# Placing on-chip buffers by their start address modulo 256 bytes in a two-layer encoder trunk

## The chip, the core and the metric

The kernel runs on one core of a Trainium2 chip. The metric is the device time of one execution in microseconds (us); lower is better. TensorE (PE) multiplies, VectorE (DVE) and ScalarE (ACT) work on elements, GpSimd (POOL) and SyncE (SP) mostly issue DMAs. A matmul has two operands in the on-chip memory: a stationary one of 128 columns, which a weight load (PEld) brings into the array first, and a moving one of up to 512 columns, which then streams through it. In a row of the trace "out<-moving,stationary" is the order.

## The reference

One even and one odd layer on 1024 tokens of width 1024, all in float32, cut to what matters:

```python
def even_mixer(x, ...):          # layer 0
    c_q, c_kv, k_r, f = split(x @ w_in)
    q = rms_norm(c_q) @ w_uq;  k, v = rms_norm(c_kv) @ (w_uk, w_uv)     # 8 heads
    p = softmax((q_nope @ k_nope.T + rot(q_rope) @ rot(k_r).T) * scale)
    return concat([p @ v, fft2(f).real]) @ w_out
def odd_mixer(x, ...):           # layer 1
    u, v = split(gelu(x @ w_in))
    s = einsum('gpq,bnqgc->bnpgc', w_s, chunks(layer_norm(v))) + b_s
    return (u * s) @ w_out
for layer in range(2):
    x = layer_norm(alpha * x + mixer(x))
    x = layer_norm(alpha * x + (silu(x @ w_gate) * (x @ w_up)) @ w_down)
```

## The kernel before

Every float32 operand is split into a high and a low part (`split`, one ACT copy and one DVE subtraction) and every product is made of three matmuls (`mm3`: high by high, high by low, low by high). The big products use a seven-product block scheme (`seven`, `reduce`, `v_pair`).

The stages follow each other in time: the input projection (`even_front`, 0 to 139 us of the profiled span), the Fourier part and the attention (139 to 570), `reduce` of the mixer, the feed-forward of layer 0 (`ffn`, 712 to 1137), its `reduce`, the v half (`v_pair`, 1372 to 1532) and the u half (`spatial`, 1532 to 1757) of layer 1, its `reduce`, the feed-forward of layer 1 (1934 to 2359) and the last `reduce`.

Tiles come from pools, which are stacked from the left end of the memory upwards (`side` "left") or from the right end downwards; what is opened earlier shifts what is opened later. The start addresses modulo 256, as the built program has them, are the same on every partition. "Gap" below is the moving operand's start minus the stationary one's, modulo 256.

| matmuls | stage | moving at | stationary at | gap |
|---|---|---|---|---|
| 3648 of `xo`/`xa` by `whi`/`wlo` of pool wts, 512 columns | feed-forward, u half | 32 | 160 | 128 |
| 720 of the same by `whi`/`wlo` of pool wtx | feed-forward | 32 | 32 | 0 |
| 3000 of `xo` by `xo` | `reduce` | 32 | 32 | 0 |
| 312 of `cq`/`ckv` by `whi`/`wlo` | attention | 32 | 160 | 128 |
| 480 of `xT` by `whi`/`wlo` | input projection | 224 | 160 | 64 |
| 48 of `whi`/`wlo` by `gh`/`gl`, 512 columns (and a few by `gm`) | Fourier | 160 | 192 | 224 |
| 384 of `kh`/`kl` by `qh`/`ql` | scores (L1242) | 224 | 224 | 0 |
| 256 of `krh`/`krl` by `qs` | scores (L1242) | 32 | 224 | 64 |
| 768 of `pth`/`ptl` by `vh`/`vl`, 256 columns | probabilities by values | 224 | 224 | 0 |
| 1104 of `whi`/`wlo` by `xo`/`xa`, 256 columns | v half (L847) | 160 | 32 | 128 |
| 336 of the same with pool wtx | v half (L847) | 32 | 32 | 0 |
| 192 of `whi`/`wlo` by `ckv`, 256 columns | values | 160 | 32 | 128 |
| 512 transposes, stationary `p` | attention (L1261) | 128 | 224 | 160 |

In the feed-forward stages and the v half weight pairs are dealt in turn from five, one of pool wtx and four of pool wts (`more_weights`, `wpair`); the u half takes pool wts alone (`less_weights`). One unit of `seven` takes four pairs: three for two products each, the fourth for one, of twelve matmuls each.

Of the kernel before, what the change touches and what calls it, by code (L numbers as in the profile page):

```python
# [9 lines left out]
F32 = mybir.dt.float32  # L10
# [5 lines left out]
P = 128  # L16
# [18 lines left out]
def tables():  # L35
    inv = np.float32(1.0) / (np.float32(10000.0) ** (np.arange(0, ROPE, 2, dtype=np.float32) / np.float32(ROPE)))
    ang = np.arange(S, dtype=np.float32)[:, None] * inv.astype(np.float32)[None, :]
    c, s = np.cos(ang).T, np.sin(ang).T
    rope_c = np.concatenate([c, c, c, c], 0).astype(np.float32)
# [22 lines left out]
def layouts(i):  # L62
# [5 lines left out]
    def cols(w, width=P, kn=8):  # L68

        k, n = w.shape  # L70
        w = w.reshape(k // (kn * P), kn, P, n // width, width).transpose(3, 0, 2, 1, 4)
        return c(w.reshape(-1, P, kn * width))
# [16 lines left out]
        "w_in": cols(w_in),  # L89
        "g_q": c(f["even_q_norm"][0].reshape(3, P).T),  # L90
        "g_kv": c(f["even_kv_norm"][0].reshape(2, P).T),
        "w_uqr": c(rope),
# [4 lines left out]
        "o_v": cols(o_in[:, SGU:], 256, 4),  # L97
        "o_gT": c(f["odd_sgu_norm_g"][0].reshape(16, P).T),
        "o_bT": c(f["odd_sgu_norm_b"][0].reshape(16, P).T),
        "o_ws": c(f["odd_w_spatial"][0].transpose(2, 0, 1).reshape(P, 8 * P)),  # L100
# [12 lines left out]
class Trunk:  # L113
# [8 lines left out]
    def pool(self, name, side, bufs=1):  # L122
        return self.tc.tile_pool(name=self.name(name), bufs=bufs, side=side, reuse_waits="tile")


    def sub(self, out, a, b):
        self.nc.vector.tensor_tensor(out, a, b, op=ALU.subtract)  # L127
# [91 lines left out]
    def run(self):  # L219
        tc, nc, a = self.tc, self.nc, self.a  # L220
        with ExitStack() as top:
            dr = top.enter_context(tc.tile_pool(name="dram", bufs=1, space=bass.MemoryType.DRAM))
            cp = top.enter_context(self.pool("const", "left"))
            self.open_weights(top, 3, 4)
            self.small = top.enter_context(self.pool("small", "left", bufs=4))
            self.ident = cp.tile([P, P], F32, name="ident")
            make_identity(nc, self.ident)
            self.ones = cp.tile([P, P], F32, name="ones")
            nc.vector.memset(self.ones, 1.0)
            nc.scalar.copy(self.small.tile([P, 1], F32, tag="nm", name="warm"), self.ones[:, 0:1])  # L230
            self.mhalf = cp.tile([P, 8], F32, name="mhalf")
            nc.vector.memset(self.mhalf, -0.5)
            D_ = lambda n, s, k: [dr.tile(s, F32, name=f"{n}{i}") for i in range(k)]
            mix = D_("mix", [P, S], 12)
            xs = [D_(f"xs{k}_", [P, D], NT) for k in range(3)]
            self.stage = {}

            def stage(n, W, H):
                k = len(W) // 2
                self.stage[n] = {"W": W, "H": H, **{x: D_(f"{n}{x}_", [P, D], k) for x in ("SA", "SB", "TA", "TB")}}  # L240
            order = [8, 9, 10, 11, 0, 1, 2, 3, 4, 5, 6, 7]
            stage("mix", [a["w_out"][k] for k in order], [mix[k] for k in order])
            stage("odd", [a["o_out"][j] for j in range(16)], D_("tp", [P, S], 16))
            for l in range(2):
                stage(f"ffn{l}", [a["w_down"][l, j] for j in range(22)], D_(f"h{l}_", [P, S], 22))
            self.vd = D_("vd", [P, NT, 256], 8)
            self.ahead = None
            with ExitStack() as fs:
                self.ps = fs.enter_context(tc.tile_pool(name="psum", bufs=2, space=bass.MemoryType.PSUM, reuse_waits="tile"))
                self.even_front(mix)  # L250
            with ExitStack() as ms:
                self.pb = ms.enter_context(tc.tile_pool(name="psumb", bufs=1, space=bass.MemoryType.PSUM, reuse_waits="tile"))
                self.turns, self.stamp = 0, [0] * 8
                self.wx = ms.enter_context(self.pool("wtx", "left"))
                self.rcycle, self.rcount = [(self.wp, self.wbufs[0])] * self.wbufs[0] + [(self.wx, 1)], 0
                xp = ms.enter_context(self.pool("xops", "left"))
                self.xo = tuple(xp.tile([P, 5, 2, 4, 256], F32R, name=f"xo{x}") for x in "hl")
                self.xa = None
                self.mp = ms.enter_context(self.pool("main", "right"))
                x_in = [a["x"][t * P:(t + 1) * P, :] for t in range(NT)]  # L260
                gate_up = lambda l: lambda j: (a["w_gate"][l, j], a["w_up"][l, j])
                w0 = {}

                def pre(l):
                    self.less_weights()
                    w0[l] = [self.right_operands(*gate_up(l)(0))]
                    self.more_weights()
                    w0[l].append(self.right_operands(*gate_up(l)(1)))

                def pre_v():  # L270
                    self.less_weights()
                    w0["v"] = self.v_begin(0)
                    self.more_weights()
                G = self.stage
                pend = self.reduce(G["mix"], x_in, None, (0, 0), xs[0], self.ahead, lambda: pre(0))
                self.ffn(w0[0], gate_up(0), G["ffn0"], pend)
                pend = self.reduce(G["ffn0"], xs[0], (0, 0), (0, 1), xs[1], None, pre_v)
                left = self.spatial(w0["v"], G["odd"], pend)
                pend = self.reduce(G["odd"], xs[1], (0, 1), (1, 0), xs[2], None, lambda: pre(1), left)
                self.ffn(w0[1], gate_up(1), G["ffn1"], pend)  # L280
                self.reduce(G["ffn1"], xs[2], (1, 0), (1, 1), None)
                self.xpool.__exit__(None, None, None)
# [617 lines left out]
    def even_front(self, mix):  # L900
        nc, a = self.nc, self.a
        col = lambda i: self.unit(a["w_in"][i], 8)
        with ExitStack() as keep:
# [7 lines left out]
            gq = cn.tile([P, 3], F32, name="gq")  # L911
            gkv = cn.tile([P, 2], F32, name="gkv")
            with ExitStack() as fs:
                fp = fs.enter_context(self.pool("fefo", "left"))
                fe = [fp.tile([P, 512], F32, name=f"fe{i}") for i in range(FG)]
                fo = [fp.tile([P, 512], F32, name=f"fo{i}") for i in range(FG)]
# [154 lines left out]
    def fourier(self, fe, fo, f512, chan, mix):  # L1071
# [2 lines left out]
        nc, a = self.nc, self.a  # L1074
        H = FD // 2
        with ExitStack() as es:
            gp = es.enter_context(self.pool("gf", "right"))
            T = lambda shape, dt, name: gp.tile(shape, dt, name=self.name(name))
            pair = lambda shape, name: (T(shape, F32R, name + "h"), T(shape, F32R, name + "l"))
# [89 lines left out]
    def attention(self, cq, ckv, kr, rc, rs, mix):  # L1169
        nc, a = self.nc, self.a  # L1170
        with ExitStack() as es:
            ap = es.enter_context(self.pool("attn", "right"))
            T = lambda shape, dt, tag, bufs=1: ap.tile(shape, dt, tag=tag, name=self.name(tag), bufs=bufs)
            st = {}

            def weights(hp):

                st[hp] = {"ur": self.unit(a["w_uqr"][hp], 3), "un": self.unit(a["w_uqn"][hp], 3), "ukv": self.unit(a["w_ukv"][hp], 2)}
# [116 lines left out]
            for i in range(len(items) + 3):  # L1295
# [6 lines left out]
                if i < len(items):  # L1302
# [7 lines left out]
                    left = max(1, NT - 1 - qt)  # L1310
# [24 lines left out]
```

## Time and profile before

| what | value |
|---|---|
| median of three runs | 2599.66 us (2596.24 to 2603.76) |
| profiled execution | 2598.74 us, of which the span of its instructions 2597.0 us |
| mean granted TensorE clock | 0.981 |
| busy: PE, PEld, DVE, ACT, POOL | 96%, 80%, 71%, 41%, 12% of the span |
| matmuls | 12294 |

The page's busy share of PE counts modelled ends, which overlap the next start; how long a matmul holds the engine is read from the starts of those that follow each other without idle time.

### The profile page before, as it was taken

To read this page: it belongs to the slowest core of one execution; us is meant where nothing else is said; L and a number is where in the kernel's file an instruction comes from. 1 tells how busy PE (TensorE), PEld (TensorE's weight loads), DVE (VectorE), ACT (ScalarE), POOL (GpSimd) and SP (SyncE) were. 2 spreads that over 40 slices of the span, in tenths; PEclk is the share of its full clock that TensorE was granted. 3 is DMA by queue.
4 is the path that set the end of the run, shared out by engine and by line. 5 is a ranking of instruction groups with operands and counts; after the bars stand their busy time and mean duration, and the time that the engine had idled before them with its cause. 6 is when DMAs were issued, how large, how long until landed. Compare 5 with 4: busy or idle time off the path is not lost. (4 is left out here: it accounts for less than half of the span.)

```text
span 2597.0 us, 33135 instructions
## 1 busy us (share of the span) xinstructions
PE 2491.1 (96%) x12294; PEld 2087.2 (80%) x12294; DVE 1841.1 (71%) x2673; ACT 1077.2 (41%) x1643; POOL 309.3 (12%) x504
## 2 busy tenths in 40 slices
PE   8989999989899999999999999898999999998997
PEld 7878888877778888878889997776877888887886
DVE  4448878757886666668687867788787666666767
ACT  4225555544643333334356432232474333333332
POOL 1000111010111111110011223230010101111001
PEclk9989999999999999999999999999999999999998
DMA  4122333148343454477645644476624534538654
GB/s 172 42 87 70 137 114 110 53 152 287 117 143 141 171 179 149 151 285 249 202 163 187 218 158 147 138 251 237 230 105 146 179 137 170 184 140 320 204 185 142
DMA packets 164073, 431.95 MB, mean 166 GB/s; under 512 B 19880, under 2 KB 26696, under 8 KB 163912
## 3 DMA queue, kind: packets, MB, share of 16 engines
q1 hardware_dynamic: 108216, 232.11, 27.1%
q0 software_dynamic: 55696, 197.73, 20.4%
q8 instruction: 96, 1.57, 0.3%
q14 instruction: 65, 0.53, 0.1%
HBM read 286.64 MB, written 138.41 MB: 164 GB/s over the span
## 5 line engine op out<-in xcount | busy, mean ns | idle before, releaser
L137 PE MATMUL b<-xoh,whi 128*128 128x512 f32 x1040 | 413.9, 398 | 20.1 <-ACT whi L131 18.2
L131 ACT CAST xoh<-rx 128x1024 fp32r<-128x1024 f32 (+1 forms) x264 | 255.0, 1006 | 424.6 <-PE b L138 323.2
L132 DVE TENSOR_TENSOR xol<-rx,xoh 128x1024 fp32r<-128x1024 f32 (+1 forms) x264 | 299.5, 1160 | 165.8 <-ACT xoh L131 165.1
L138 PE MATMUL b<-xol,xoh 128*128 128x512 f32 x1000 | 394.6, 395 | 19.3 <-DVE xol L132 19.3
L139 PE MATMUL b<-xoh,wlo 128*128 128x512 f32 x1040 | 411.1, 396 | 0.6 <-DVE wlo L132 0.2
L138 PE MATMUL b<-xol,whi 128*128 128x512 f32 x1040 | 410.8, 395 | 0.0
L137 PE MATMUL b<-xoh 128*128 128x512 f32 x1000 | 390.0, 396 | 21.5 <-ACT xoh L131 21.5
L131 ACT CAST whi<-raw 128x1024 fp32r<-128x1024 f32 (+3 forms) x265 | 250.5, 953 | 373.8 <-PE b L138 220.1
L132 DVE TENSOR_TENSOR wlo<-raw,whi 128x1024 fp32r<-128x1024 f32 (+3 forms) x265 | 290.0, 1101 | 162.9 <-ACT whi L131 160.1
L139 PE MATMUL b<-xoh,xol 128*128 128x512 f32 x1000 | 392.9, 393 | 0.0
L137 PEld LDWEIGHTS b<-xoh,whi 128*128 128x128 f32 x1040 | 196.9, 189 | 65.7 <-ACT whi L131 19.2
L137 PEld LDWEIGHTS b<-xoh 128*128 128x128 f32 x1000 | 190.0, 191 | 63.3 <-ACT xoh L131 24.0
L138 PEld LDWEIGHTS b<-xol,xoh 128*128 128x128 f32 x1000 | 190.5, 190 | 62.5 <-DVE xol L132 23.1
L139 PEld LDWEIGHTS b<-xoh,wlo 128*128 128x128 f32 x1040 | 196.6, 189 | 48.4 <-DVE wlo L132 3.7
L138 PEld LDWEIGHTS b<-xol,whi 128*128 128x128 f32 x1040 | 197.0, 189 | 44.4 <-issue 0.2
L139 PEld LDWEIGHTS b<-xoh,xol 128*128 128x128 f32 x1000 | 190.3, 190 | 39.9
L613 ACT COPY y<-b 128x512 f32<-128x512 f32 x200 | 116.7, 588 | 226.7 <-PE b L139 221.4
L137 PE MATMUL b<-xah,whi 128*128 128x512 f32 x416 | 166.2, 399 | 0.0
L138 PE MATMUL b<-xal,whi 128*128 128x512 f32 x416 | 165.2, 397 | 0.0
L139 PE MATMUL b<-xah,wlo 128*128 128x512 f32 x416 | 163.5, 394 | 0.0
L127 DVE TENSOR_TENSOR raw<-raw,raw 128x512 f32<-128x512 f32 (+1 forms) x172 | 126.9, 738 | 25.9 <-DMA raw<-w_up 21.4
L658 DVE TENSOR_TENSOR y<-b,y 128x512 f32<-128x512 f32 x84 | 57.9, 690 | 102.0 <-PE b L139 102.0
(376 smaller groups left out, 4523.6 us busy)
## 6 DMA issues: line engine op xcount, KB each, us to landing
raw<-w_gate SPq DMA_DIRECT2D x44, 512.0 KB, 3.5
raw<-w_up SPq DMA_DIRECT2D x44, 512.0 KB
q<-w_down POOLq DMA_DIRECT2D x44, 512.0 KB, 4.9
h<-x POOLq DMA_DIRECT2D x44, 512.0 KB, 3.7
rx<-h SPq DMA_DIRECT2D x66, 256.0 KB, 3.0
rx<-w_down SPq DMA_DIRECT2D x66, 256.0 KB, 5.1
raw<-o_v SPq DMA_DIRECT2D x16, 512.0 KB, 4.9
x<-o_out POOLq DMA_DIRECT2D x16, 512.0 KB, 6.2
```

Source lines behind the costliest of these rows:

```text
L127: self.nc.vector.tensor_tensor(out, a, b, op=ALU.subtract)
L131: a = self.nc.scalar.copy(hi, src)
L132: return a.ins, self.nc.vector.tensor_tensor(lo, src, hi.bitcast(F32), op=ALU.subtract).ins
L137: mm(ps, lh, rh, start=start, stop=False, skip_group_check=skip)
L138: mm(ps, lh, rl, start=False, stop=False, skip_group_check=skip)
L139: mm(ps, ll, rh, start=False, stop=stop, skip_group_check=skip)
L613: nc.scalar.copy(t, ps)
L658: self.last_v = nc.vector.tensor_tensor(sb, ps, sb, op=op).ins
```

## The change

The pool `small` is opened ahead of the weights' pool wts, so wts starts 128 bytes further on modulo 256. A helper `shift` takes a tile of n bytes that nothing uses, and clears it once on POOL; seven such tiles move what is placed after them.

```diff
+    def shift(self, pool, n):
+        self.nc.gpsimd.memset(pool.tile([P, n // 4], F32, tag=self.name("pad"), name=self.name("pad"), bufs=1), 0.0)
...
             cp = top.enter_context(self.pool("const", "left"))
+            self.small = top.enter_context(self.pool("small", "left", bufs=4))
             self.open_weights(top, 3, 4)
-            self.small = top.enter_context(self.pool("small", "left", bufs=4))
...
             with ExitStack() as fs:
+                self.shift(fs.enter_context(self.pool("top", "right")), 224)
...
         with ExitStack() as es:
+            self.shift(es.enter_context(self.pool("gap", "right")), 96)
             gp = es.enter_context(self.pool("gf", "right"))
...
         with ExitStack() as es:
+            self.shift(es.enter_context(self.pool("top", "right")), 192)
             ap = es.enter_context(self.pool("attn", "right"))
-            T = lambda shape, dt, tag, bufs=1: ap.tile(shape, dt, tag=tag, name=self.name(tag), bufs=bufs)
+            pads = {"kh0": 32, "vh": 64, "qh1": 160, "kh1": 32}
             st = {}
+
+            def T(shape, dt, tag, bufs=1):
+                n = pads.pop(tag, 0)
+                if n:
+                    self.shift(ap, n)
+                return ap.tile(shape, dt, tag=tag, name=self.name(tag), bufs=bufs)
```

In the built program the starts modulo 256 are then: `whi`/`wlo` of both pools 32, `xT` 0, `q` and `qs` 0, `k` 32, `pt` 32, `v` 96, `p` 96, `gh` 128; `xo`, `xa`, `cq`, `ckv` and `kr` stay at 32. So the gap is 0 for all 4368 matmuls of the feed-forward and u stages, for the 312 of `cq`/`ckv`, all 1440 of the v half and the 192 of the values; 32 for all 640 of the scores; 224 for the 480 of `xT`; 192 for the 768 of the probabilities by the values; 160 for those of `gh`; 32 for the transposes of `p`.

The order of instructions on PE, DVE, ACT and SP is what it was. On POOL the seven clears are new. Its rows around the Fourier part and the first pair of heads, before (`altf` is the Fourier part's first load, `rw` the rotated query half that the first scores need):

```order
L1085 DMA altf_1158<-t_alt 1x16x32
L1086 DMA altcf_1160<-t_altc 128x2
L330 DMA raw_1754<-w_out 128x1024
L330 DMA raw_1755<-w_out 128x1024
L1035 TENSOR_TENSOR rw_1445<-rw_1445,rope_s 128x512
```

The same place with the change; the clear of 24 columns waits for PE, as the load behind it did before, and the one of 40 columns waits for a matmul of the Fourier part:

```order
L127 MEMSET pad_1157 128x24
L1091 DMA altf_1168<-t_alt 1x16x32
L1092 DMA altcf_1170<-t_altc 128x2
L334 DMA raw_1779<-w_out 128x1024
L334 DMA raw_1780<-w_out 128x1024
L127 MEMSET pad_1529 128x8
L127 MEMSET pad_1551 128x16
L127 MEMSET pad_1643 128x40
L127 MEMSET pad_1707 128x8
L1040 TENSOR_TENSOR rw_1462<-rw_1462,rope_s 128x512
```

One clear now stands ahead of the Fourier part's loads and four ahead of the first product with `rw`; the other two stand near the program's start.

## Rows read from the trace of the kernel before

**Rows 1.** Stretches: length, then busy us and instructions by engine, granted clock, DMA.
```profile
core 0: us, PE busy (x) PEld busy (x) DVE busy (x) ACT busy (x) POOL busy (x), PEclk, DMA share, GB/s
139.00:570.00 431.00, 423.06 (x2553) 369.62 (x2552) 314.44 (x492) 209.72 (x398) 42.89 (x65) 0.98 0.29 94
712.00:1137.00 425.00, 423.90 (x1824) 344.20 (x1825) 293.07 (x405) 165.49 (x238) 46.42 (x87) 1.00 0.44 156
1372.00:1532.00 160.00, 155.50 (x1279) 154.41 (x1278) 120.50 (x193) 74.62 (x115) 39.05 (x70) 0.98 0.60 205
1532.00:1757.00 225.00, 207.23 (x981) 170.31 (x981) 174.06 (x344) 71.64 (x103) 62.02 (x94) 0.96 0.49 172
```

**Rows 2.** Timeline of PE in one feed-forward unit: start us, length us, instruction.
```profile
876.22 0.39 PE L137 MATMUL b<-xoh,whi 128*128 128x512 f32 x1
...
881.66 0.40 PE L137 MATMUL b<-xoh,whi 128*128 128x512 f32 x1
...
889.80 0.40 PE L139 MATMUL b<-xoh,wlo 128*128 128x512 f32 x1
```

**Rows 3.** Waits of ACT in the feed-forward of layer 0: total, times, longest.
```profile
ACT whi L131 <- PE b L138: 106.2, 55, 2.2
```

**Rows 4.** Timeline of PE in the attention, products of cq.
```profile
226.44 0.39 PE L137 MATMUL mm<-cq0h,whi 128*128 128x512 f32 x1
...
230.38 0.39 PE L139 MATMUL mm<-cq2h,wlo 128*128 128x512 f32 x1
```

**Rows 5.** Timeline of PE in the v half.
```profile
1480.69 0.28 PE L847 MATMUL b<-whi,xoh 128*128 128x256 f32 x1
...
1486.43 0.28 PE L847 MATMUL b<-whi,xoh 128*128 128x256 f32 x1
...
1492.01 0.28 PE L847 MATMUL b<-whi,xol 128*128 128x256 f32 x1
```

**Rows 6.** Timeline of PE in the Fourier part.
```profile
153.27 0.40 PE L138 MATMUL S<-wlo,gh 128*128 128x512 f32 x1
...
158.40 0.40 PE L139 MATMUL S<-whi,gl 128*128 128x512 f32 x1
```

**Rows 7.** Timeline of PE in one block of scores and the instruction after it.
```profile
389.77 0.39 PE L1242 MATMUL S<-kl,qh 128*128 128x512 f32 x1
...
391.87 0.40 PE L137 MATMUL mm<-ckv0h,whi 128*128 128x512 f32 x1
```

**Rows 8.** Timeline of PE in the input projection.
```profile
57.95 0.40 PE L138 MATMUL mm<-xT,whi 128*128 128x512 f32 x1
...
68.48 0.39 PE L139 MATMUL mm<-xT,wlo 128*128 128x512 f32 x1
```

**Rows 9.** Timeline of PE, probabilities by values.
```profile
394.50 0.28 PE L137 MATMUL mm<-pth,vh 128*128 128x256 f32 x1
...
396.90 0.28 PE L139 MATMUL mm<-pth,vl 128*128 128x256 f32 x1
```

**Rows 10.** Groups by line and form: count, busy us and mean ns, idle before.
```profile
L132 DVE TENSOR_TENSOR xol<-rx,xoh 128x1024 fp32r<-128x1024 f32 x236 | 281.2, 1216 | 153.3 <-ACT xoh L131 152.7 <-DMA rx<-mix 0.2
L132 DVE TENSOR_TENSOR wlo<-raw,whi 128x1024 fp32r<-128x1024 f32 x203 | 246.8, 1221 | 146.4 <-ACT whi L131 143.6 <-PE b L359 1.1
L1261 PE MATMUL mm<-ident,p 128*128 128x128 f32 x512 | 66.1, 272 | 0.0
L137 PEld LDWEIGHTS mm<-pth,vh 128*128 128x128 f32 x256 | 48.7, 190 | 0.9 <-ACT pth L131 0.5 <-DVE ptl L132 0.4
L359 PE MATMUL b<-ident,x 128*128 128x128 f32 x120 | 15.3, 273 | 0.4 <-DVE q L436 0.4
```

**Rows 11.** Timeline of POOL at the start and at the first rw product.
```profile
0.74 0.20 POOL masks.py:197 MEMSET ident<- 128x128 f32 x1 [0.29 <-POOLq L1327]
177.99 1.26 POOL L1035 TENSOR_TENSOR rw<-rw,rope_s 128x512 f32<-128x512 f32 x1 [23.89 <-DMA rw<-rt]
```

**Rows 12.** Timeline of PE at the end of the Fourier part.
```profile
159.62 0.28 PE L1137 MATMUL mm<-gl,altc 128*2 128x256 f32 x1
```

## The prediction

> **What bounds the kernel now.** I read the stretches first, then the starts of single matmuls, then the waits. In the feed-forward of layer 0 PE is busy 423.90 of 425.00 us, in the attention 423.06 of 431.00, in the v half 155.50 of 160.00 and in the u half 207.23 of 225.00; DVE and ACT are well below it in each, the DMA share is at most 0.60 [rows 1]. Where ACT stands idle in the feed-forward, it is mostly for PE to free a weight pair: 106.2 us in 55 waits [rows 3]. So the time per matmul on PE sets the time of these stages. The feed-forward of layer 1 is the same code, and I count it like that of layer 0. The four `reduce` stages multiply operands that the change doesn't move against each other; I leave them as they are.
>
> The reader should then look at how far apart the starts of matmuls lie within one unit. From 876.22 to 881.66 us stand 24 matmuls whose weights come from pool wtx, the gap between operands being 0: 5.44 us / 24 = 226.7 ns each. From 881.66 to 889.80 follow, without a break, matmuls of the same lines and sizes, whose weights come from pool wts (gap 128): 35 intervals in 8.14 us = 232.6 ns each [rows 2]. The granted clock of the stage is 1.00, the 2.4 GHz level, at which 512 columns are 213.3 ns. Both kinds lose time beyond the columns; the one with the gap of 128 loses 5.9 ns more. This is the change's own experiment, already in the kernel before.
>
> **The terms.** *Feed-forward.* Each of the two stretches has 1824 matmuls of 512 columns [rows 1], 1464 of them with the gap of 128. 2 x 1464 x 5.9 ns = 17.3 us less. *u half:* 672 matmuls, all with the gap of 128, 672 x 5.9 = 4.0 us less. Here PE is idle 18 us [rows 1], and waits there could take the gain; I take it whole, since the stage's chain runs through PE again after each wait, and use 0 as the other bound. The last 48 of the 3648 stand ahead of the two feed-forward stretches (24 each): 0.3 us less.
>
> *Products of cq and ckv.* 226.44 to 230.38 us is 17 intervals, 231.8 ns [rows 4]; to 226.7 that is 5.1 ns, for 312 of them 1.6 us less.
>
> *Columns of 256, gap 128 to 0.* In the v half 48 matmuls with gap 0 take 1480.69 to 1486.43, 119.6 ns each, and with gap 128 the 47 intervals to 1492.01 are 118.7 ns [rows 5]. So here likeness costs 0.9 ns: (1104 + 192) x 0.9 = 1.2 us more.
>
> *Scores, gap 0 and 64 to 32.* A block's nine intervals from 389.77 to 391.87 are 233.3 ns each [rows 7]. No row has a gap of 32. Bounds: 226.7 as for gap 0 [rows 2], and 233.2 as for the gap of 224, which is 32 the other way (158.40 - 153.27 over 22 intervals, [rows 6]). 32 lies between 0 and 64, and gap 64 has 228.9 ns in `xT` [rows 8] but is part of the 233.3 here, so I take the middle, 230.0: 640 x 3.3 = 2.1 us less; from 4.2 less to 0.
>
> *xT, gap 64 to 224.* 57.95 to 68.48 is 46 intervals, 228.9 ns [rows 8]. The bounds are the same two, 226.7 and 233.2; the middle is 1.1 above: 480 x 1.1 = 0.5 us more; from 1.1 less to 2.1 more. The row of gap 224 speaks for the upper end, but its operands stand at 192 and 160, and the new ones at 32 and 0, so I don't take it as settled.
>
> *Probabilities by values, gap 0 to 192.* Now 394.50 to 396.90 is 20 intervals, 120.0 ns [rows 9]. No row has 256 columns at 192. The nearest is gap 128, 118.7 [rows 5]: 768 x 1.3 = 1.0 us less. Bounds: no loss at all, 256 columns at 2.4 GHz = 106.7 ns, 10.2 us less; and the largest loss of a 512-column row, 233.3 - 213.3 = 20 ns, on 106.7, that is 126.7: 5.1 us more.
>
> *Nothing else.* Transposes of `p` go from gap 160 to 32; at gap 160 they are 272 ns and at 128 273 ns long [rows 10], and 1 ns of 512 is 0.5 us either way. The 48 by `gh` move between gaps of unlike operands. DVE's subtraction is 1216 ns with all at 32 and 1221 with most at 160 [rows 10], so element work doesn't care. The seven clears: 128 columns took 0.20 us on POOL [rows 11], and the largest has 56. The one that waits is released by a matmul of the Fourier part, at the latest the one at 159.62 us [rows 12]; the product of `rw` queued behind it starts at 177.99 because its DMA is late [rows 11]. That DMA hides the clears; without it the four would cost under 0.8 us once. The clear ahead of the Fourier part's loads waits for PE as they did.
>
> Sum: -17.3 - 4.0 - 0.3 - 1.6 + 1.2 - 2.1 + 0.5 - 1.0 = -24.6 us. Against the profiled execution, 2598.74 us (0.9 below the median of the runs shown; its span is 2597.0), that is 2574.1, so 2574 us.
>
> **A rule that speaks against it.** [rows 2] shows two placements with different times at the same operation. The Trainium skill, page "SBUF — State Buffer", section "A bandwidth-pool intuition that's wrong (but worth ruling out)", gives PE a second, independent read port for weight loads, and its section "SBUF: two separate sides" says that PE's ports never wait on anyone; by it the start addresses would not matter and the time would stay 2598.7. By that rule, the trace disagrees: 232.6 against 226.7 ns.
>
> **Rivals.** (1) *Placement isn't the cause* of those 5.9 ns but, say, the pool's place in the cycle: then 2598.7. For it: two ports could be independent. Against it: the jump from 226.7 to 232.6 stands at the very matmul at which the pool changes, with the products before and after alike, and `reduce`'s timing isn't needed for it. (2) *Unlike small gaps cost in full:* scores stay at 233.2, xT goes to 233.2, values to 126.7, with the sure terms -17.3 - 4.0 - 0.3 - 1.6 + 1.2: -22.0 + 0 + 2.1 + 5.1 = -14.8, 2584 us. [rows 6] speaks for its xT part. (3) *Small gaps are as good as none and the values stream freely:* -22.0 - 4.2 - 1.1 - 10.2 = -37.5, 2561 us. For it only that 0 and 32 are near each other; nothing in the trace shows 106.7 ns. (4) *Waits take half:* another engine or a DMA becomes late in the u half and the feed-forward, as weight pairs are asked for earlier, and keeps half of 17.3 + 4.0: -24.6 + 10.7 = -13.9, 2585 us. Against it DVE's 293 of 425 us and the DMA share of 0.44 [rows 1], and ACT waiting for PE [rows 3]. (5) *Slower:* a weight load takes 190 ns [rows 10] and lies behind earlier matmuls of 120 ns. If a gap of 192 ended that overlap in the 768 products with the values, each would take up to 190 ns: 768 x 70 = 54 us more, less 23.6 elsewhere, 2629 us. It decides from 120 + 23.6 us / 768 = 151 ns on. Against it: no row of any gap loses more than 20 ns on its columns.
>
> **How the numbers follow.** The sum's own case 0.48 (its range 2568 to 2582), (2) 0.21, (3) 0.20, (4) 0.05, (1) 0.04, (5) 0.02. From 2561 to 2588 reach the cases of the same mechanism with the u half's gain lost (4.0 on 2584); with 2 us for the spread of the runs I give 2559 to 2590, which leaves out (1), (5) and the tails. A measurement of this kernel can tell about 0.3%, 7.8 us, from no change: faster 0.94, the same 0.04, slower 0.02.
>
> **What would show it.** In the profile after, starts of `xoh,whi` in any feed-forward unit should be 226.7 ns apart throughout, and both feed-forward stages some 8.7 us shorter; the v half about 0.5 us longer in its matmuls; products of `cq` at 226.7. The starts of scores, xT and `pth,vh` settle the three open terms. ACT's waits for PE should still be the largest in the feed-forward. The prediction is wrong if `xoh,whi` stays at 232, if the values rise over 130 ns, or if PE's waits in the u half grow by what its matmuls save.

## The result, and the profile after

| | before | with the change |
|---|---|---|
| median | 2598.79 us (4 runs, 2596.24 to 2603.76) | 2582.49 us (4 runs, 2579.81 to 2583.88) |
| profiled execution, its span | 2598.74, 2597.0 us | 2581.6, 2579.8 us |
| mean granted clock | 0.981 | 0.981 |

The ratio is 0.9934 with an interval of 0.9916 to 0.9951, so the change is worth 16.3 us, with an interval of 12.7 to 21.8. It is faster, inside the range given; the forecast gain was 24.6 us.

The first view is the table of stretches of the kernel with the change, one row per stage and each cut at its first matmul; the columns are those of [rows 1].

```profile
0.00:131.19 131.19, 124.14 (x520) 97.57 (x521) 54.52 (x92) 44.82 (x63) 8.48 (x15) 1.00 0.31 106
131.19:573.09 441.90, 423.99 (x2611) 370.75 (x2610) 321.22 (x512) 215.67 (x412) 46.36 (x75) 0.98 0.31 101
...
709.35:1126.01 416.66, 415.65 (x1825) 343.25 (x1825) 292.43 (x405) 164.20 (x238) 46.39 (x87) 1.00 0.44 158
...
1362.37:1523.12 160.75, 156.33 (x1276) 155.45 (x1273) 120.83 (x193) 74.03 (x113) 39.22 (x71) 0.98 0.59 205
1523.12:1750.56 227.44, 209.18 (x983) 172.93 (x981) 174.02 (x343) 71.48 (x103) 61.85 (x93) 0.94 0.49 170
...
1928.07:2344.68 416.61, 415.61 (x1824) 343.16 (x1825) 292.69 (x405) 164.01 (x238) 45.32 (x85) 1.00 0.46 161
```

Against the kernel before both feed-forward stages are 8.4 us shorter (425.0 before, 416.7 now), with the instructions and nearly the DMA share they had. The v half is 0.7 to 1.2 us longer. The u half is not shorter but 2.4 us longer, at a granted clock of 0.94 instead of 0.96. The input projection took 129.0 and now 131.2. Attention with the Fourier part took 449.1 us in the trace of before, cut in the same way, and now 441.9:

```profile
129.00:578.10 449.10, 432.35 (x2612) 378.13 (x2610) 321.35 (x512) 215.77 (x412) 46.02 (x70) 0.97 0.30 99
```

Not all of these 7.2 us is the change's: the stage's time at half the granted clock, 1.2 GHz, was 26 us in the trace of before and 17 in that of the change.

The second view is the timeline of PE, two rows (the first and the last of a stretch without idle time) for a feed-forward unit, `xT`, a block of scores, products of `cq`, two stretches of the probabilities by the values, and the v half. Columns as in [rows 2].

```profile
860.13 0.39 PE L141 MATMUL b<-xoh,whi 128*128 128x512 f32 x1
...
871.69 0.39 PE L141 MATMUL b<-xoh,whi 128*128 128x512 f32 x1
...
59.03 0.39 PE L142 MATMUL mm<-xT,whi 128*128 128x512 f32 x1
...
69.29 0.40 PE L141 MATMUL mm<-xT,whi 128*128 128x512 f32 x1
...
393.15 0.39 PE L1255 MATMUL S<-kh,qh 128*128 128x512 f32 x1
...
395.24 0.39 PE L1255 MATMUL S<-krl,qs 128*128 128x512 f32 x1
...
382.90 0.39 PE L141 MATMUL mm<-cq0h,whi 128*128 128x512 f32 x1
...
384.71 0.39 PE L143 MATMUL mm<-cq2h,wlo 128*128 128x512 f32 x1
...
390.64 0.28 PE L143 MATMUL mm<-pth,vl 128*128 128x256 f32 x1
...
393.03 0.28 PE L143 MATMUL mm<-pth,vl 128*128 128x256 f32 x1
...
228.56 0.28 PE L142 MATMUL mm<-ptl,vh 128*128 128x256 f32 x1
...
231.27 0.39 PE L1255 MATMUL S<-kh,qh 128*128 128x512 f32 x1
...
1469.72 0.28 PE L851 MATMUL b<-whi,xol 128*128 128x256 f32 x1
...
1482.32 0.28 PE L851 MATMUL b<-whi,xol 128*128 128x256 f32 x1
```

Read in that order: 51 intervals of 226.7 ns, through three pairs of weights from both pools, where [rows 2] had a step to 232.6; 44 intervals of 233.2 for `xT` ([rows 8]: 228.9); nine of 232.2 for the scores, where [rows 7] had 233.3; eight of 226.3 for `cq` ([rows 4]: 231.8); 21 of 113.8 and 23 of 117.8 for the values, two speeds of the same instructions ([rows 9]: 120.0); 105 of 120.0 in the v half ([rows 5]: 119.6 and 118.7).

ACT's waits in the feed-forward of layer 0 (total us, times, longest) are still mostly for PE, as in [rows 3]:

```profile
ACT whi L135 <- PE b L142: 102.9, 54, 2.1
```

### The profile page after: what moved, and what is told of

Read it like the earlier page. It is cut to its first block, busy times and chain, and to the rows that moved or that the text cites. A ratio compares the mean times of both kernels' runs of the same rounds, so it can differ in the third digit from the quotient of the medians.

```text
span 2579.8 us, 33141 instructions
## 1 busy us (share of the span) xinstructions
PE 2470.9 (96%) x12294; PEld 2081.9 (81%) x12294; DVE 1840.4 (71%) x2673; ACT 1074.4 (42%) x1643; POOL 309.8 (12%) x511
## 3 DMA queue, kind: packets, MB, share of 16 engines
q0 software_dynamic: 55696, 197.73, 20.6%
## 5 line engine op out<-in xcount | busy, mean ns | idle before, releaser
L135 ACT CAST xoh<-rx 128x1024 fp32r<-128x1024 f32 (+1 forms) x264 | 255.1, 1006 | 425.7 <-PE b L142 324.3
```

Source lines behind the costliest of these rows:

```text
L135: a = self.nc.scalar.copy(hi, src)
```

## The experiments

Every run has the reference's whole computation. "One execution" is a single profiled one; the other times are medians of several, against the kernel before on the same chip. Stages are cut at their first matmul, as above. The gap is still the moving operand's start minus the stationary one's, modulo 256.

**The weights' pool alone.** The pool is moved as in the change; the seven cleared tiles are left out.

```diff
+            self.small = top.enter_context(self.pool("small", "left", bufs=4))
             self.open_weights(top, 3, 4)
-            self.small = top.enter_context(self.pool("small", "left", bufs=4))
```

> The weights' pool alone is moved (the pool small ahead of it), no pad anywhere. Theory: the gap between stationary and moving operand sets a matmul's time. Then starts of xoh,whi in the feed-forward lie 226.7 ns apart, each feed-forward stage is 416 to 417 us as with the whole change, cq/ckv by whi are near 228 ns, the values stay at 120.0 ns and the scores at 232 to 233, xT (gap now 192) is anywhere in 227 to 234; the time is 2598.8 - 16.9 - 1.5 + 1 = about 2581 to 2586, the u half deciding within that. Rival (the pads matter as much, or it is where the weights' pool ends and not the gap): the feed-forward stays at 425 us and the time within 5 us of the kernel before.

Measured: 2585.48 us against 2605.82, ratio 0.9922 (0.9902 to 0.9941). Three stretches of its trace, the input projection and the two feed-forwards:

```profile
0.00:131.27 131.27, 124.17 (x520) 97.41 (x521) 54.52 (x92) 44.81 (x63) 8.24 (x12) 1.00 0.31 106
...
710.42:1128.10 417.68, 416.67 (x1825) 343.97 (x1825) 292.54 (x405) 164.10 (x238) 46.55 (x87) 0.99 0.45 158
...
1931.26:2347.89 416.63, 415.62 (x1824) 343.21 (x1825) 292.61 (x405) 164.12 (x238) 45.46 (x85) 1.00 0.46 161
```

This one moved line gives the feed-forward's whole gain and, within the intervals, that of the whole change. It also lengthens the input projection to 131.27 us: with the weights at 32, `xT` is at a gap of 192. The change's own pad turns that into 224, and nothing is won by it (131.19). One expectation missed: products of `cq` and `ckv`, at gap 0 here as in the change, take 230.0 ns on average and not near 228 (228.1 in the change).

**The values alone**, before with two pads, so that only the probabilities by the values change their gap, from 0 to 192.

```diff
+            pads = {"vh": 64, "qh1": 192}
```

> The kernel before with the values alone 64 bytes on (and the other heads' tiles 256 on, so at the same place modulo 256): gap 192 for the 768 products of probabilities and values, all else as before. Theory: 114 to 115 ns apart as with the whole change, against 120.0 before, so the attention is 3.5 to 4 us shorter and nothing else moves. Rival: the 115 ns come from the probabilities standing at 32 instead of 224, or from a neighbour (transposes, scores) and not from the gap: then they stay at 120.

One execution: 2595.26 us, the kernel before on that chip 2605.82. First and last row of a stretch of 23 intervals, and the feed-forward:

```profile
202.42 0.28 PE L142 MATMUL mm<-ptl,vh 128*128 128x256 f32 x1
...
205.04 0.40 PE L1252 MATMUL S<-kh,qh 128*128 128x512 f32 x1
```

```profile
706.51:1132.02 425.51, 424.51 (x1825) 344.65 (x1826) 293.18 (x405) 165.65 (x238) 46.41 (x87) 0.99 0.44 155
```

The values take 113.9 ns here and the feed-forward is as before: moving this group alone gives this group's gain. Over all their stretches the values have 114.4 ns, against 119.7 at gap 0. (That neighbours have no effect at all isn't shown; the version with everything at gap 0, below, speaks against it.)

**Gaps in steps of 32.** The four weight pairs of wts lie 32 bytes apart, so one program has four gaps; from the changed kernel they are 32, 64, 96 and 128, from the kernel before 160, 192, 224 and 0. (`rstd` moves to pool `small` to make room.)

```diff
+            t = pool.tile([P, 2056], F32R, tag="w", name=self.name("whi"), bufs=bufs)
+            return t[:, :1024], t[:, 1024:2048]
```

> The changed kernel with the four weight pairs of pool wts 32 bytes apart modulo 256 (at 32, 64, 96, 128; the left operands then stand at 160, the pool wtx pair too), so that one execution has matmuls of 512 columns at the gaps 128, 96, 64, 32 and 0, and of 256 columns at 128, 160, 192, 224 and 0. Theory (the gap alone): 226.7 ns at 0, 232.5 at 128, each gap with its own figure; at 32 231 to 233 as in the scores, and 256 columns at 192 have the 114 to 115 ns of the values. Rival (granules of 64 bytes: only which 64-byte piece counts): 32 reads like 0 or like 64, whichever piece it falls in. Rival (only likeness counts): every gap but 0 reads 232.5, and 256 columns read 118.7 at all of them.

> The kernel before with the four weight pairs of pool wts 32 bytes apart modulo 256 (at 160, 192, 224, 0; the left operands at 160), so gaps of 0, 224, 192 and 160 for 512 columns and of 0, 32, 64 and 96 for 256 columns. Theory (the gap alone, with its sign): 226.7 at 0, about 233 at 224 as in the Fourier part and in xT of the changed kernel; 256 columns at 64 need not read like those at 192. Rival (only the distance counts): 224 reads like 32, 192 like 64, 160 like 96 of the other kernel with steps, and 256 columns at 64 read 115 like those at 192.

One execution each: 2601.84 and 2601.75 us. Timeline of PE in the feed-forward of the first, three pieces of 24 intervals, at gaps 64, 96 and 32:

```profile
743.36 0.39 PE L141 MATMUL b<-xoh,whi 128*128 128x512 f32 x1
...
748.86 0.39 PE L141 MATMUL b<-xah,whi 128*128 128x512 f32 x1
...
754.31 0.39 PE L141 MATMUL b<-xoh,whi 128*128 128x512 f32 x1
...
759.91 0.39 PE L141 MATMUL b<-xoh,whi 128*128 128x512 f32 x1
...
768.20 0.40 PE L141 MATMUL b<-xah,whi 128*128 128x512 f32 x1
...
773.79 0.39 PE L141 MATMUL b<-xoh,whi 128*128 128x512 f32 x1
```

229.2, 233.3 and 232.9 ns: the same lines and the same pool, and only the start differs. A small gap is no good as such: 32 costs as much as 128, which agrees with the scores, the term that the prediction left open, and 64 costs less than its neighbours. The feed-forwards took 426.4 us in this kernel and 424.8 and 425.7 in the other.

**Gaps in steps of 32, 16 bytes on**, by slices of the same tile.

```diff
+            return t[:, 4:1028], t[:, 1028:2052]
```

> As steps_from_32, the weights 16 bytes further on: gaps of 112, 80, 48 and 16 for 512 columns, 144, 176, 208 and 240 for 256 columns, and 0 from pool wtx. Theory (the gap in granules of 32 bytes or finer): 16 lies off 0 and reads 230 to 234 like 32; of 256 columns none reads below the 114 of gap 192. Rival (granules of 64 bytes, of which the operand's place counts): 16 reads 226.8 like 0, and 48 like 32.

> As steps_from_160, the weights 16 bytes further on: gaps of 240, 208, 176 and 144 for 512 columns, 16, 48, 80 and 112 for 256 columns. Theory: 512 columns read 232 to 235 at all of them, 240 included. Rival: 240 (16 the other way) reads 226.8, so that likeness need not be exact.

One execution each: 2589.84 and 2598.95 us. Two pieces of 24 intervals of the first, at gaps 48 and 16:

```profile
741.68 0.39 PE L141 MATMUL b<-xoh,whi 128*128 128x512 f32 x1
...
747.25 0.40 PE L141 MATMUL b<-xah,whi 128*128 128x512 f32 x1
...
766.62 0.40 PE L141 MATMUL b<-xah,whi 128*128 128x512 f32 x1
...
772.09 0.39 PE L141 MATMUL b<-xoh,whi 128*128 128x512 f32 x1
```

and two of the second, both at gap 240:

```profile
719.73 0.39 PE L137 MATMUL b<-xah,whi 128*128 128x512 f32 x1
...
725.17 0.39 PE L137 MATMUL b<-xah,whi 128*128 128x512 f32 x1
...
792.80 0.40 PE L137 MATMUL b<-xah,whi 128*128 128x512 f32 x1
...
798.40 0.39 PE L137 MATMUL b<-xoh,whi 128*128 128x512 f32 x1
```

232.1 and 227.9 ns, then 226.7 and 233.3 ns at one and the same gap. So 16 is nearly as good as 0, and at some gaps a stretch runs at one of two speeds. Both theories missed, the first at 16 and the second at 240. The rival of the first read 16 and 48 rightly, but not the whole: pieces of 64 bytes would also make 48 and 80 alike, and they are not.

The table puts the fourteen traces together: for every stretch of at least nine intervals without idle time I took the mean of its intervals between starts, and list the means that hold more than a twentieth of the intervals, rounded to 1 ns.

| gap | 512 columns, ns | 256 columns, ns | gap | 512 columns, ns | 256 columns, ns |
|---|---|---|---|---|---|
| 0 | 227 to 228 | 119 to 120 | 128 | 232 to 233 | 118 to 119 |
| 16 | 227 to 229 | 113 to 114 or 119 | 144 | 232 to 233 | 119 |
| 32 | 232 to 234 | 117 to 118 | 160 | 234 | 117 to 120 |
| 48 | 231 to 232 | 118 to 119 | 176 | 231 to 232 | 119 |
| 64 | 229 to 230 | 118 | 192 | 233 | 113 to 114 or 118 |
| 80 | 230 | 120 | 208 | 233 | 119 to 120 |
| 96 | 233 to 234 | 119 to 120 | 224 | 233 | 118 |
| 112 | 227 or 233 to 234 | 114 to 118 | 240 | 227 or 233 to 234 | 117 to 118 |

It is the gap that counts and not where the operands stand: 512 columns at gap 128 have 232.4 ns with the moving operand at 32 and the stationary one at 160 (the kernel before), and 232.8 with these two places exchanged (steps of 32 from the changed kernel); at gap 0 they have 227 ns with both at 32 and with both at 160.

**The same two kernels again**, as one execution each, for how far stages differ between executions.

> The kernel before once more, for how far a stage's length moves between executions. Theory: the first profile's u half (225.0 us, with 17 us at half clock in four pieces) was a short one; where the pieces at half clock fall differs from run to run, and this one reads 226 to 229 us, with matmuls of xoh,whi at 232.4 ns as before. Rival (the change made the u half longer by its own doing): 225 us again, with the same four pieces.

> The changed kernel once more. Theory: as in the first, feed-forward stages of 416.6 us, xT at 233.3 and scores at 233 ns; the u half anywhere in 223 to 228 us, longer by about half of what its time at half clock is longer. Rival: 227.5 again with 27 us at half clock, so that the placement itself costs the u half its 4 us.

2607.18 and 2582.16 us. The u half of the kernel before, now at a clock of 0.95:

```profile
1535.87:1764.98 229.11, 211.05 (x983) 173.33 (x981) 173.97 (x343) 71.57 (x103) 62.06 (x93) 0.95 0.49 169
```

It took 225.0 us in the first profile [rows 1] and 229.1 in this one. Inside it stand pieces at half the granted clock, 1.2 GHz. The kernel with the change has one of them at 1658.30 us; the stretch ahead of it and the piece:

```profile
1650.00:1658.30 8.30, 6.13 (x36) 5.18 (x34) 7.67 (x22) 0.00 (x0) 1.99 (x3) 1.00 0.79 283
1658.30:1668.50 10.20, 6.42 (x14) 4.68 (x15) 5.51 (x8) 2.99 (x4) 3.45 (x5) 0.50 0.60 203
```

PE was busy 6.13 of 8.30 us there, after a stretch without idle time (10.00 of 10.00 us from 1640.00 on), and then the clock fell to 0.50. Such pieces add up to 17 us in the first profile of before, 24 in the second, and 27 in the first two of the changed kernel; in these four they start at the same places of the stage (some 47, 74, 136 and 160 us in, within 4 us), and two more (108 and 197) were missing in the first profile of before alone. It happened to be a good one, and the comparison of the u halves by the two first profiles misleads.

The changed kernel read as its rival said, 227.5 us with 27 at half clock. That the placement costs the u half 4 us doesn't follow, since the kernel before was at 229.1 by then. A third profile of the changed kernel (from the timed run further on) has 24 us at half clock, as much as the second of before, and is 2.3 us shorter than it:

```profile
1522.41:1749.23 226.82, 208.46 (x982) 172.92 (x981) 173.68 (x343) 71.50 (x103) 61.77 (x93) 0.95 0.49 171
```

The weights' pool alone had 226.9 us, and the values alone, whose u half is that of before, 228.3, each with 24 us at half clock too. So at like clock the u half is 1.4 to 2.3 us shorter. Whether the placement itself adds to the half-clock time isn't shown: 27 us stood only in kernels whose u half has gap 0 or 64, in four of seven profiles, and 17 to 24 in the seven others.

**Everything at gap 0**, the change with other pads, so that `xT` and the scores have gap 0 too, and the values keep 192.

```diff
-                self.shift(fs.enter_context(self.pool("top", "right")), 224)
+                self.shift(fs.enter_context(self.pool("top", "right")), 192)
-            self.shift(es.enter_context(self.pool("gap", "right")), 96)
+            self.shift(es.enter_context(self.pool("gap", "right")), 224)
-            pads = {"kh0": 32, "vh": 64, "qh1": 160, "kh1": 32}
+            pads = {"vh": 64, "qh1": 192}
```

> The changed kernel with other pads alone: gap 0 also for xT by whi, for all five products of the scores, and for whi by gh; the values keep 192. Theory (only a gap of 0 is cheap for 512 columns): 480 x (233.3 - 227.0) + 640 x (232.7 - 227) + 48 x 6 = 3.0 + 3.7 + 0.3 = 7 us less than the changed kernel, about 2575.5, or 0.9907 of the kernel before. Rival (scores cost 232 for another reason, since products of q and k with a gap of 0 in the kernel before read 230 to 234): only xT falls, 3 us less, 2579.5.

2582.21 us against 2600.39, ratio 0.9927 (0.9909 to 0.9944): no better than the change. The expected 2575.5 did not come, and the rival missed too, since the scores did get shorter. Timeline of a block of scores, first, sixth and tenth matmul, and of a stretch of the values:

```profile
378.51 0.40 PE L1255 MATMUL S<-kh,qh 128*128 128x512 f32 x1
...
379.67 0.39 PE L1255 MATMUL S<-kh,qh 128*128 128x512 f32 x1
...
380.58 0.39 PE L1255 MATMUL S<-krl,qs 128*128 128x512 f32 x1
```

```profile
203.97 0.28 PE L142 MATMUL mm<-ptl,vh 128*128 128x256 f32 x1
...
206.68 0.40 PE L1255 MATMUL S<-kh,qh 128*128 128x512 f32 x1
```

The first five scores of a block take 232 ns each and only then 227.5: a block of ten is too short to profit in full. The values are at 117.8 ns, the slower of their two speeds, in 28 of their 32 stretches: a mean of 117.4 over all, where the change had 115.1, which costs 768 x 2.3 ns = 1.8 us and eats what the scores gain (their mean is 229.7, against 232.8). The values' own starts are those of the change, which had 11, 11 and 9 slower stretches in its three profiles, eight of them the same ones; the version below, with the same attention as here, had 30 in both of its profiles. So their speed goes with the program around them and is not chance alone. Which part of it counts (the scores' gap is one that changed) isn't shown. The input projection is at 129.0 us again, with 227.2 ns for `xT`.

**The v half at gap 192 too.** `xo` and its companion `xa` are placed 64 bytes further on ahead of the v half, and `xo` is put back after the u half, so that the v half's 256 columns have 192 and the u half's 512 columns 64. (`xa` moves with `xo`, whose tile is now 64 bytes longer; the `shift` of 192 puts `xa` back for the feed-forwards.)

```diff
-                self.xo = tuple(xp.tile([P, 5, 2, 4, 256], F32R, name=f"xo{x}") for x in "hl")
+                xo = xp.tile([P, 20496], F32R, name="xoh")
+                self.place = lambda o: setattr(self, "xo", tuple(xo[:, i + o:i + o + 10240].rearrange("p (o b k c) -> p o b k c", o=5, b=2, k=4) for i in (0, 10240)))
+                self.place(0)
...
+                self.place(16)
...
+                self.place(0)
...
+        if rgb != (0, 0):
+            self.shift(xa, 192)
```

> As alike_all, and the left operands stand 64 bytes on (at 96) from the reduce of the first feed-forward to the end of the u half, so that the v half's 1440 matmuls of 256 columns have the gap 192, and the u half's 672 of 512 columns the gap 64. Theory: 120.0 to 114.7 ns in the v half, 7.6 us less; 226.8 to 229.3 in the u half, 1.6 us more; about 2569.5, or 0.9884 of the kernel before. Rival (the v half waits for others by then: its DMA share is 0.60 and DVE 121 of 160 us busy): its matmuls read 114.7, but the stage stays within 2 us of 160.7 and the time with alike_all's.

> The changed kernel, timed beside v_half_timed on one chip. Theory: ratio to the kernel before 0.993 to 0.994 as in the first runs, feed-forward stages 416.7 us and the u half 227.4. Rival: the first ratio was chance and this one lies below 0.991 or above 0.996.

> The version with the v half at the gap 192, timed once more. Theory: 3.0 us from xT, 2.5 us from the v half and 1 to 2 from the rest less than the changed kernel, a ratio of 0.990 to 0.992 to the kernel before. Rival: the 10 us that it was ahead of alike_all were chance, since only its v half differs by 2.5 us; then it stands at 0.993 like the changed kernel.

First, beside the run above: 2571.44 us against 2600.39, ratio 0.9897 (0.9879 to 0.9915). Then the change and this version together on one other chip, each against the kernel before at 2602.16 us: 2582.41 us, 0.9923 (0.9910 to 0.9935), and 2571.76 us, 0.9876 (0.9861 to 0.9891), beyond the expected 0.990 to 0.992. It beats both kernels, the change by 10.6 us. (The expected 7.6 us for the v half took 1440 matmuls; the built program has 1344 there, of which 240 and not 336 had pool wtx before.)

The v half of the change, and of this version in its two profiles:

```profile
1362.22:1522.41 160.19, 155.97 (x1275) 154.98 (x1274) 120.82 (x193) 74.04 (x113) 39.20 (x71) 0.98 0.59 205
```

```profile
1361.91:1520.10 158.19, 152.86 (x1276) 151.62 (x1274) 120.39 (x193) 74.13 (x113) 38.97 (x70) 0.98 0.60 207
```

```profile
1364.13:1519.94 155.81, 149.22 (x1275) 147.79 (x1274) 119.43 (x190) 73.60 (x113) 38.55 (x69) 0.98 0.61 210
```

The last two are one program. In the first profile this stretch, 354 intervals, ran at 117.8 ns:

```profile
1403.69 0.28 PE L857 MATMUL b<-wlo,xah 128*128 128x256 f32 x1
...
1445.38 0.28 PE L857 MATMUL b<-wlo,xoh 128*128 128x256 f32 x1
```

and in the second the same place, 350 intervals, at 113.3:

```profile
1406.82 0.28 PE L857 MATMUL b<-whi,xal 128*128 128x256 f32 x1
...
1446.49 0.28 PE L857 MATMUL b<-wlo,xoh 128*128 128x256 f32 x1
```

So at gap 192 the speed is not settled by the placement; a stretch keeps one of the two from its first few matmuls to its end. The shorter v half is 2.0 and 4.4 us of the 10.6. The input projection, with `xT` at gap 0, is another 3.5: 127.4 and 127.3 us in the two profiles, against 130.8 in the change on the second chip. In the second:

```profile
0.00:127.31 127.31, 120.35 (x520) 96.74 (x521) 54.51 (x92) 44.84 (x63) 8.48 (x15) 1.00 0.32 109
```

The `reduce` after the u half is at 174.2 us in both and at 176.6 in the change, but the kernel in half steps from 160, which doesn't have this edit, had 173.9 too. Together that is 8 to 10 us.

In the total of the profiled executions (2579.9 and 2579.6 us, the longest of their runs) most of it is lost again: attention with the Fourier part took 446 us there, with 26 and 24 us at half clock, against 441.0 with 11 in the change. The other runs had a mean granted clock of 0.981 to 0.983 where these two had 0.977 and 0.978. At 0.981 two runs of this version took 2571.8 us and six of the change 2579.8 to 2583.9, so the distance to the change isn't one of clock. The distance to everything at gap 0 is so in part: that kernel's two runs at 0.981 and 0.983 took 2577.8 and 2575.4 us, the four at 0.978 to 0.980 took 2581.4 to 2585.3.

## Why the prediction was right, and what was mis-sized

The mechanism held. The Trainium skill, page "SBUF — State Buffer", section "SBUF: two separate sides", says that PE's ports never wait on anyone; what the prediction drew from it, that the starts would not matter, is not what these runs show: moving one pool gave 0.9922. Rival (1), placement not the cause, falls by that run and by the steps of 32, in which the pool's place in the cycle stays and the time changes with the start. Rival (4), waits, falls for the feed-forward: ACT's waits for PE are 102.9 us (106.2 in [rows 3]) and the stage kept all that its matmuls gained. PE's idle time in the u half didn't grow by what its matmuls saved, which would have been a sign of being wrong: 17.8 us before ([rows 1]) and 18.3 with the change. Rival (5), a lost overlap of weight loads, falls: the values became faster. Rivals (2) and (3) were each half right, (2) on `xT` and the scores, (3) partly on the values.

Term by term, with the means over all intervals of a kind in the first profiles of before and after, which are slightly above single stretches:

| term | forecast, us | measured, us | from |
|---|---|---|---|
| feed-forward | -17.3 | -16.8 | two stages, 425.0 to 416.7 and 425.0 to 416.6 |
| u half | -4.0 | -2.7 | some 600 intervals at full clock, 232.3 to 227.8 ns |
| 48 others | -0.3 | not read | |
| `cq`, `ckv` | -1.6 | -1.5 | 312 x (233.0 - 228.1) ns |
| v half and values of `ckv` | +1.2 | +1.2 | v half, 159.6 to 160.8 |
| scores | -2.1 | +0.6 | 640 x (232.8 - 231.9) ns |
| `xT` | +0.5 | +2.1 | 480 x (233.3 - 229.0) ns |
| probabilities by values | -1.0 | -3.5 | 768 x (119.7 - 115.1) ns |
| sum | -24.6 | -20.6 | |

Four terms were mis-sized. For the **scores** and **xT** the prediction took the middle between the gap of 0 and that of 224, and both came out at the upper bound, 232.8 and 233.3 ns: [rows 6] had the right value for 224, and the step of 32 shows the same for 32. That nearness to 0 counts for something was the wrong thought there; it cost 4.3 us of the forecast. Nor was the lower bound within reach for the scores: with everything at gap 0 they have 229.7 ns on average and not 226.7. The **values** came out better than the nearest row, gap 128, since 192 has a second, faster speed; they gave back 2.5. For the **u half** the step that failed was to take 5.9 ns for every matmul: the intervals at full clock fell by 4.5 ns, and their mean is 227.8 ns instead of 226.7 (its stretches are short; that this is why is not shown); of the other matmuls 43 ran at 1.2 GHz and 36 ended in a break (15 and 38 in the first profile of before).

The sum of -20.6 lies inside the timed interval, 12.7 to 21.8 us. Between the first two profiles the span fell by 17.2 us, less than the sum, and three differences make that up, none of them a term. The u half is 2.4 us longer instead of 2.7 shorter, with 27 us at half clock instead of 17 (at like clock it is 1.4 to 2.3 us shorter, as shown above). Attention with the Fourier part is 7.2 us shorter where its terms give 4.4, with 17 us at half clock instead of 26. The four `reduce` stages together are 1.2 us longer. That the measured 16.3 us lies in the range owes something to the range's width and to luck: a third of the forecast gain of 24.6 did not come, and the values made up for part of what the scores and `xT` lost. The second timing of the change, 2602.16 to 2582.41, gave 19.8 us.

Not settled: what picks one of the two speeds at a gap of 192, 112 or 240, what shortens the `reduce` after the u half in the version with the v half, and whether the placement has a part in the time at half clock.

## What to carry to other kernels

Where PE sets the time and matmuls of one line have two durations at full clock, compare the start addresses of their operands modulo 256 before anything else: here 512-column float32r products took 226.7 ns with equal starts and up to 234 without, and opening one pool before another moved 0.8% of the time. The best gap depends on the width (0 for 512 columns; for 256 here 192, and 112, untried as a placement, had 114 to 116 ns in most of one trace's intervals), so place by operand and check each product kind by the starts of its matmuls, short blocks apart from long ones. A term between two bounds should be taken at the bound that a row with the same gap shows, and stages with pieces at half clock should be compared over more than one profile.

## What the runs showed of the hardware that was not expected

- The time of a matmul depends on the gap, but doesn't grow with its size: at 512 columns 0 and 16 give 227 to 229 ns, 32 gives 232 to 234, 64 and 80 give 229 to 230. It has a sign: 64 is 229 to 230 and 192 is 233, 16 is 227 to 229 and 240 either 227 or 233.
- Some gaps have two speeds in one trace, about 113.5 and 117.8 ns (256 columns, gap 192) or 227 and 233 (512 columns, gaps 112 and 240). In the v half at gap 192 one program kept 117.8 over 354 intervals in one execution and 113.3 over 350 at the same place in another. The values, with their own starts unchanged, had 9 to 11 slower stretches of 32 in three profiles of one program and 28 to 30 in three of two others.
- A block of ten scores at gap 0 (everything at gap 0) needs about five matmuls to come down from 232 to 227.5 ns.
